# First stage of a trunk kernel: latents ahead of context, with a written order for three k tiles

## The chip, the cores and the metric

The kernel runs on one core of a Trainium2 chip. The metric is the device time of one execution in microseconds (us); the reader sees the median of three runs and one execution that the hardware profiler recorded. Engines are named as in the profile: PE is TensorE (PEld its weight loads), DVE is VectorE, ACT is ScalarE, POOL is GpSimd and SP is SyncE, which issues nearly all DMA transfers here. A "q" behind an engine's name means its sequencer.

## The reference

A trunk of two layers works on 256 latent tokens `x` and 256 context tokens `ctx`, both of width 2048. Of each layer, what matters here is its beginning:

```python
shift, scale, gate = jnp.split(silu_c @ w_mod[l] + b_mod[l], 3, axis=-1)
shift_c, scale_c, gate_c = jnp.split(silu_cc @ w_mod[l] + b_mod[l], 3, axis=-1)

h = rmsnorm(x, g_pre[l]) * (1.0 + scale[:, None]) + shift[:, None]
h_c = rmsnorm(ctx, g_pre[l]) * (1.0 + scale_c) + shift_c
proj = h @ w_in[l]
proj_c = h_c @ w_in[l]
```

Both streams are normalised over the 2048 features, scaled and shifted by a modulation computed from `silu(c)` and `silu(c_ctx)`, and projected with the same weights `w_in`. The columns of the projection feed a gated MLP (parts called au, av, ag), windowed attention (q, k, v, bg) and a Fourier branch (cx, cg); their outputs are joined and projected by `w_out`. All of it is in float32.

## The kernel before

Activations lie transposed: features on the 128 partitions, in 16 tiles of 128 features (k tiles, `KT`), and tokens along the free axis, 256 latents and then 256 context tokens (`T` = 512, `S` = 256). `yo[k]` holds x and ctx of k tile k. Each float32 product is made from three passes of a reduced type: every operand is split into a high and a low part (`hh`/`hl` for activations, `whi`/`wlo` for weights), and `mm3` multiplies high by high, high by low and low by high. ACT makes a high part, DVE the low one. `W`, the `Stream`, loads weight blocks of 128x1024 into `raw` (three buffers) and splits them into `whi` and `wlo`; `emitting(512)` does so by halves.

The first stage of layer 0 runs over the k tiles. For every k tile, the modulation's scale and shift come from 2 MB of `w_mod` (`in_wsl_dram`), read in four quarters by the generator `mod_start`: one `next` issues the loads, four multiply a quarter each on PE (`ps_mod`, L169), one transposes on DVE, the last multiplies once more (`ps_modc`, L178) and writes `gs` (scale) and `sh` (shift). Odd k tiles load into the buffers mg, mgl, hh, hl (from k tile 9 on yo in place of hh, hl), even ones into mraw, mraw, macc, vv. `make_h` then forms h on DVE (L507), its high part on ACT (L511) and its low part on DVE (L516), and PE multiplies it into av (four tiles of 128 tokens, `start_av`) and into three heads of au (`start_au`). All these sums stay in PSUM for the whole stage.

Ahead of the stage stand the statistics. SP loads all of x and ctx, ACT squares each `yo[k]` (L1238), and PE sums the squares over the partitions by products with ones (L1242), which go to four column groups of the array in turn. The sums are copied, added up (L1254), scaled on DVE, raised to -1/2 on POOL, and spread to all partitions by a broadcast product (`bcast`, `ps_rb`). Products with zeros (`warm`, L474, `ps_idle`) fill PE between these pieces; I call them fillers.

PE's order is the order in which the program is written (`manual_schedule`), and in the first stage the same holds for DVE, ACT and SP. Each queue runs in order: an instruction that waits holds up all that stand behind it on its engine. Two constants shape the steps: up to k tile `EARLY` a step computes the modulation of the next k tile, from there on that of the one after the next; in step `EARLY` itself there are two. `LOADS` and `SPLITS` say how many weight blocks are loaded and split in each step.

## Time and profile before

| what | value |
|---|---|
| median of 3 runs (lowest to highest) | 1136.24 us (1136.19 to 1136.27) |
| the profiled execution | 1136.23 us |
| its span, first to last instruction | 1134.5 us |
| PE busy in the span | 1122.2 us (99%) |
| first projection (av) of k tile 0 | at 24.57 us |
| first projection of k tile 1 | at 33.66 us |
| first stage's last au product ends, next unit starts | at 138.51 us |

A timeline row reads: start, time from the first start to the last end, engine, line, operation, output<-inputs, shape, count, and in brackets how long the engine had been idle and what released it. Matmuls are pipelined and their ends modelled, so a matmul's duration is longer than the distance to the next one; distances of starts tell PE's pace. A row of windows gives for each engine the busy time and the number of instructions.

### The profile page before, as it was taken

To read this page: it belongs to the slowest core of one execution; us is meant where nothing else is said; L and a number is where in the kernel's file an instruction comes from. 1 tells how busy PE (TensorE), PEld (TensorE's weight loads), DVE (VectorE), ACT (ScalarE), POOL (GpSimd) and SP (SyncE) were. 2 spreads that over 40 slices of the span, in tenths; PEclk is the share of its full clock that TensorE was granted. 3 is DMA by queue.
4 is the path that set the end of the run, shared out by engine and by line. 5 is a ranking of instruction groups with operands and counts; after the bars stand their busy time and mean duration, and the time that the engine had idled before them with its cause. 6 is when DMAs were issued, how large, how long until landed. Compare 5 with 4: busy or idle time off the path is not lost.

```text
span 1134.5 us, 16841 instructions
## 1 busy us (share of the span) xinstructions
PE 1122.2 (99%) x6332; PEld 932.0 (82%) x6335; DVE 879.7 (78%) x1480; ACT 514.6 (45%) x933; POOL 33.0 (3%) x39
## 2 busy tenths in 40 slices
PE   8999999999999999999999999999999999999997
PEld 3567788888898888888888888988898988888885
DVE  1545499999987887789999994397788689868884
ACT  5322422322325667632533323366555369856551
POOL 0000000000000000000000000205000000000001
PEclk9999999999999999999999999999999999999998
DMA  9999666556655343356466664269656686555872
GB/s 353 400 390 403 241 204 191 179 189 219 207 168 184 113 136 117 116 188 188 166 203 212 215 196 157 62 192 240 203 182 208 214 273 191 175 163 188 299 261 74
DMA packets 72659, 234.28 MB, mean 207 GB/s; under 512 B 8449, under 2 KB 11393, under 8 KB 72577
## 3 DMA queue, kind: packets, MB, share of 16 engines
q1 hardware_dynamic: 70272, 231.11, 61.1%
q0 software_dynamic: 2304, 2.10, 1.2%
q8 instruction: 49, 0.80, 0.3%
q14 instruction: 34, 0.27, 0.1%
HBM read 231.08 MB, written 2.10 MB: 206 GB/s over the span
## 4 chain that ended last, share of the span: by engine, by line
PE 97%; DMA 2%; DVE 0%; SPq 0%; ACT 0%; issue 0%; POOL 0%; DVEq 0%; POOLq 0%
PE ps_t L428 14%; PE ps_t L429 14%; PE ps_t L430 14%; PE ps_t L545 10%; PE ps_t L546 5%; PE ps_y L428 3%; PE ps_y L430 3%; PE ps_y L429 3%; PE ps_mod L169 2%; PE ps_av L428 2%; PE ps_cx L428 2%; PE ps_cx L430 2%; PE ps_cx L429 2%; PE ps_av L429 2%; PE ps_av L430 2%; PE ps_tp L924 2%
## 5 line engine op out<-in xcount | busy, mean ns | idle before, releaser
L403 ACT CAST whi<-raw 128x1024 fp32r<-128x1024 f32 (+1 forms) x216 | 224.0, 1041 | 328.8 <-PE ps_t L429 182.1
L408 DVE TENSOR_TENSOR wlo<-raw,whi 128x1024 fp32r<-128x1024 f32 (+1 forms) x216 | 260.4, 1210 | 62.9 <-ACT whi L403 61.5
L428 PE MATMUL ps_t<-hh,whi 128*128 128x512 f32 (+1 forms) x704 | 268.4, 381 | 0.0
L430 PE MATMUL ps_t<-hh,wlo 128*128 128x512 f32 (+1 forms) x704 | 267.8, 380 | 0.0
L429 PE MATMUL ps_t<-hl,whi 128*128 128x512 f32 (+1 forms) x704 | 267.6, 380 | 0.0
L207 DVE SCALAR_TENSOR_TENSOR macc<-mraw,cs,macc 128x512 f32<-128x512 f32 x360 | 249.1, 746 | 17.1 <-DMA mraw<-in_wmod_dram 17.1
L545 PE MATMUL ps_t<-hh,whi 128*128 128x512 f32 x448 | 163.7, 403 | 0.0
L430 PEld LDWEIGHTS ps_t<-hh,wlo 128*128 128x128 f32 x704 | 132.5, 188 | 25.2
L428 PEld LDWEIGHTS ps_t<-hh,whi 128*128 128x128 f32 x704 | 132.5, 188 | 24.7 <-issue 0.8
L429 PEld LDWEIGHTS ps_t<-hl,whi 128*128 128x128 f32 x704 | 132.5, 188 | 23.4
L546 PE MATMUL ps_t<-hh,wlo 128*128 128x256 f32 x448 | 125.7, 281 | 0.0
L545 PEld LDWEIGHTS ps_t<-hh,whi 128*128 128x128 f32 x448 | 84.3, 188 | 19.1 <-issue 0.5
L546 PEld LDWEIGHTS ps_t<-hh,wlo 128*128 128x128 f32 x448 | 84.9, 189 | 0.5 <-issue 0.5
L511 ACT ACTIVATE hh<-w2k,sh 128x256 fp32r<-128x256 f32 x48 | 21.8, 502 | 79.2 <-DVE w2k L507 79.2
L428 PE MATMUL ps_y<-whi,hh 128*128 128x512 f32 x104 | 41.3, 397 | 0.0
L430 PE MATMUL ps_y<-whi,hh 128*128 128x512 f32 x104 | 40.6, 391 | 0.0
L429 PE MATMUL ps_y<-wlo,hh 128*128 128x512 f32 x104 | 40.5, 390 | 0.0
L428 PE MATMUL ps_av<-whi,hh 128*128 128x512 f32 x96 | 39.9, 416 | 0.6 <-ACT hh L511 0.6
L428 PE MATMUL ps_cx<-whi,hh 128*128 128x512 f32 x96 | 38.7, 403 | 0.0
L429 PE MATMUL ps_av<-wlo,hh 128*128 128x512 f32 x96 | 37.9, 395 | 0.0
L429 PE MATMUL ps_cx<-wlo,hh 128*128 128x512 f32 x96 | 37.4, 389 | 0.0
L445 ACT CAST w2k<-ps_tp 128x512 fp32r<-128x512 f32 x40 | 23.4, 584 | 23.2 <-PE ps_scc L429 12.7
(398 smaller groups left out, 1858.6 us busy)
## 6 DMA issues: line engine op xcount, KB each, us to landing
raw<-in_win_dram SPq DMA_DIRECT2D x160, 512.0 KB, 4.2
mraw<-in_wmod_dram SPq DMA_DIRECT2D x128, 512.0 KB, 4.5
raw<-in_wout_dram SPq DMA_DIRECT2D x60, 512.0 KB, 4.4
mraw<-in_wsl_dram SPq DMA_DIRECT2D x16, 512.0 KB, 7.2
yo<-in_xT_dram SPq DMA_DIRECT2D x16, 256.0 KB, 5.2
macc<-in_wsl_dram SPq DMA_DIRECT2D x8, 512.0 KB, 7.8
vv<-in_wsl_dram SPq DMA_DIRECT2D x8, 512.0 KB, 7.7
mg<-in_wsl_dram SPq DMA_DIRECT2D x8, 512.0 KB, 8.0
```

The source lines that it names most:

```text
L169: PE.matmul(ps[32 * kk:32 * kk + 32, 0:n], cpad[:, kg * 4 + kk], ws[kk], start=kg == 0, stop=kg == 3, tile_position=(0, 32 * kk))
L207: V.scalar_tensor_tensor(out=acc[:, s], in0=w[:, kk % 2], scalar=c, in1=acc[:, s], op0=ALU.mult, op1=ALU.add)
L403: A.copy(ph, rc)
L408: self.last = V.tensor_tensor(out=pl, in0=rc, in1=ph.bitcast(F32), op=ALU.subtract)
L428: PE.matmul(ps, st[0], mv[0], start=start, stop=False)
L429: PE.matmul(ps, st[0], mv[1], start=False, stop=False)
L430: PE.matmul(ps, st[1], mv[0], start=False, stop=stop)
L445: A.copy(hi, src)
L511: first = A.activation(h_of(l, k, sl)[0], t[:, sl], AF.Identity, bias=sh[l][:, k, s:s + 1])
L545: PE.matmul(ps, w[0], h, start=k == 0, stop=False)
L546: PE.matmul(ps[:, 0:S], w[1], h[:, 0:S], start=False, stop=k == KT - 1)
L924: PE.transpose(tp[:, (2 * j + b) * P:(2 * j + b + 1) * P], src, ident)
```

## The change

x and ctx are loaded as separate streams, in pairs of k tiles: `yo[2i]` holds the latents of k tiles 2i and 2i+1, `yo[2i+1]` their context, and `x_of` finds them in layer 0. The latents come first, then half of the first weight block and the first modulation, then the context, then the second modulation. c is loaded by ACT's queue. The statistics are made for the latents alone; the context's squares and sums follow behind the latents' projection of k tile 0, each product with a filler ahead of it, and its statistics end behind that (`context`, called from the step of k tile 0). The first two weight blocks are loaded by halves (`loading`). The steps of k tiles 0, 1 and 2 have orders of their own. `EARLY` is 7 in place of 4, and `MIDDLE` is gone.

```diff
-    LOADS = [1, 2, 0, 2, 1, 1, 1, 1, 1, 0, 2, 0, 1, 1, 1, 0]
+    LOADS = [0, 2, 0, 2, 1, 1, 1, 1, 1, 0, 2, 0, 1, 1, 1, 0]
-    MIDDLE, EARLY = 3, 4
+    EARLY = 7
...
+    def x_of(l, k, s):
+        if l:
+            return yo[k][:, s * S:(s + 1) * S]
+        return yo[k // 2 * 2 + s][:, k % 2 * S:(k % 2 + 1) * S]
...
                 if k == 0:
-                    start_av(0, range(nt))
-                    take_in(3)
+                    start_av(0, (0, 1))
+                    state["context"](lambda: take_in(1))
+                    av.extend(mm_ps("av") for _ in range(2))
+                    au.extend(mm_ps("au") for _ in range(2))
+                    take_in(2)
+                    make_h(0, 0, rb0[:, CTX], [1])
+                    take_in(1)
                     e = W.emitting(512)
                     next(e)
+                    take_in(1)
                     next(e)
-                    take_in(2)
+                    next(state["w0"])
+                    start_av(0, (2,))
+                    mod_in(1)
+                    start_av(0, (3,))
+                    make_h(0, 1, rb0, [0, 1], state["w0"])
                     take(0, (1,))
-                    start_au(0, (0,))
-                    h_next()
-                    list(e)
-                    start_au(0, (1,))
-                    warm(au[2], 3)
+                    start_au(0, (0, 1))
+                elif k == 1:
+                    au.append(ms_ps("au"))
+                    start_av(1, (0, 1))
+                    take_in(5)
+                    avs = W.emitting(512)
+                    next(avs)
+                    start_av(1, (2,))
+                    take_in(1)
+                    start_av(1, (3,))
+                    make_h(0, 2, rb0, [0, 1], avs)
...
+        for i in range(8):
+            load_x(i, 0)
+            if i == 5:
+                DMA.dma_start(raw, const[:, 0:NFIRST])
+        DMA.dma_start(vecs, vec)
+        loads = [W.loading() for _ in range(2)]
+        next(loads[0])
+        m = mod_start(0, 1)
+        next(m)
+        for i in range(8):
+            load_x(i, 1)
+        made[1] = mod_start(1, 1)
+        next(made[1])
...
+        sq = mm_ps("rs2")
+        for i in range(8):
+            if i % 4 == 0:
+                warm(idle, 6)
+            square(sq, 0, i)()
...
+        r0 = sums_of(sq)
...
+        warm(idle, 2)
+        next(m)
+        spread(r0, 0)
+        for _ in range(2):
+            warm(idle, 3)
+            next(m)
+        warm(idle, 3)
+        next(m)
+        next(m)
+        warm(idle, 3)
+        sq = mm_ps("rs2")
+        first = square(sq, 1, 0)
+        list(m)
+        warm(idle, 4)
+        make_h(0, 0, rb0[:, LAT], [0])
...
+        def context(between):
+            first()
+            for i in range(1, 8):
+                product = square(sq, 1, i)
+                warm(idle, 1)
+                product()
+            r = sums_of(sq)
+            between()
+            spread(r, 1)
```

`square` squares one `yo` on ACT and returns the product with ones; `sums_of` copies the sums, adds them up and starts the root; `spread` broadcasts the result into one half of `rb0`.

Where the context's squares stand on ACT shows in its order. Before, all squares stand ahead of the copy of the sums, and k tile 0's h (`hh`) follows for both streams:

```order
L1238 ACTIVATE w2k_191<-yo_15_75 128x512
L1238 ACTIVATE w2k_194<-yo_16_76 128x512
L1243 CAST identr_89<-w2k_117 128x128
L1244 COPY cst_79<-w2k_117 128x34
L1246 COPY w2k_199<-ps_rs_33_123 128x512
L1261 COPY acc_241<-ps_rb_236 128x512
L403 CAST whi_264<-raw_209 128x512
L511 ACTIVATE hh_67_267<-w2k_269,sh_28_92 128x256 x2
```

After, one square of the context stands ahead of the latents' h and seven behind it, then the copy of their sums:

```order
L1301 COPY acc_149<-ps_rb_211 128x256
L1284 ACTIVATE w2k_242<-yo_2_62 128x512
L525 ACTIVATE hh_68_256<-w2k_258,sh_28_92 128x256
L1284 ACTIVATE w2k_271<-yo_4_64 128x512
L1284 ACTIVATE w2k_275<-yo_6_66 128x512
L1284 ACTIVATE w2k_279<-yo_8_68 128x512
L1284 ACTIVATE w2k_283<-yo_10_70 128x512
L1284 ACTIVATE w2k_287<-yo_12_72 128x512
L1284 ACTIVATE w2k_291<-yo_14_74 128x512
L1284 ACTIVATE w2k_295<-yo_16_76 128x512
L1291 COPY w2k_299<-ps_rs_65_241 128x512
```

What moved is the context's half of the statistics: from ahead of the first h to behind the latents' part of it.

On PE, with the sums of squares: before, a filler (join), then four products (ps_rs, from the squares w2k) to the four column groups, then fillers again, four times over.

```order
L474 MATMUL ps_idle_124<-join_95 128x512
L1242 MATMUL ps_rs_33_123<-w2k_143,ones_80 32x512
L1242 MATMUL ps_rs_33_123<-w2k_152,ones_80 32x512
L1242 MATMUL ps_rs_33_123<-w2k_155,ones_80 32x512
L1242 MATMUL ps_rs_33_123<-w2k_158,ones_80 32x512
L474 LDWEIGHTS join_95
L474 MATMUL ps_idle_124<-join_95 128x512
```

After, the latents' eight stand like that, but the context's stand on PE behind the first two av projections of k tile 0 (ps_av, from the weights whi, wlo and from hh, hl):

```order
L439 MATMUL ps_av_263<-whi_200,hl_69_257 128x512
L1286 MATMUL ps_rs_65_241<-w2k_242,ones_80 32x512
L483 LDWEIGHTS join_95
L483 MATMUL ps_idle_148<-join_95 128x512
L1286 MATMUL ps_rs_65_241<-w2k_271,ones_80 32x512
L483 LDWEIGHTS join_95
L483 MATMUL ps_idle_148<-join_95 128x512
L1286 MATMUL ps_rs_65_241<-w2k_275,ones_80 32x512
```

What moved is half of the products, from ahead of the first projection to behind its first half, and no two of that half are neighbours.

On SP, with the loads of the weight blocks (raw) and of the modulations of k tiles 2 (mraw, macc, vv) and 3 (mg, mgl and on): before,

```order
L383 DMA raw_298<-in_win_dram 128x1024
L162 DMA mraw_363<-in_wsl_dram 128x1024
L162 DMA mraw_365<-in_wsl_dram 128x1024
L162 DMA macc_367<-in_wsl_dram 128x1024
L162 DMA vv_369<-in_wsl_dram 128x1024
L383 DMA raw_371<-in_win_dram 128x1024
L383 DMA raw_373<-in_win_dram 128x1024
L162 DMA mg_445<-in_wsl_dram 128x1024
```

and after, at the same place of SP's queue, where raw_112 is the first block and raw_142 the second:

```order
L392 DMA raw_112<-in_win_dram 128x512
L162 DMA mraw_376<-in_wsl_dram 128x1024
L162 DMA mraw_378<-in_wsl_dram 128x1024
L162 DMA macc_380<-in_wsl_dram 128x1024
L162 DMA vv_382<-in_wsl_dram 128x1024
L392 DMA raw_142<-in_win_dram 128x512
L383 DMA raw_385<-in_win_dram 128x1024
L383 DMA raw_387<-in_win_dram 128x1024
L162 DMA mg_464<-in_wsl_dram 128x1024
```

What moved is the second halves of the first two blocks, to either side of the third modulation; the fourth block, raw_387, takes over the buffer of raw_112 and stands ahead of the next modulation as raw_373 did.

More of the change, by code (lines that the diff above doesn't have):

```diff
@@ L384, in load, with loading @@
             self.raws.append(r)
+        def loading(self):
+            n = len(self.raws)
+            r = sb([P, 1024], F32, "raw", NRAW)
+            self.raws.append(r)
+            for c in (slice(0, 512), slice(512, 1024)):
+                DMA.dma_start(r[:, c], self.src[n][:, c])
+                yield
         def emitting(self, cut=1024):
@@ L506, in make_h @@
             rsl = slice((s - streams[0]) * S, (s - streams[0] + 1) * S)
-            V.scalar_tensor_tensor(out=t[:, sl], in0=yo[k][:, sl], scalar=gs[l][:, k, s:s + 1],
+            V.scalar_tensor_tensor(out=t[:, sl], in0=x_of(l, k, s), scalar=gs[l][:, k, s:s + 1],
                                    in1=rb[:, rsl], op0=ALU.mult, op1=ALU.mult)
@@ L588, in layer @@
         ytmp = (lambda k: y1.get(k)) if last else ysl
-        av = [mm_ps("av") for _ in range(nt)]
-        au = [mm_ps("au") for _ in range(2)] + [ms_ps("au") for _ in range(1 - l)]
+        av = [mm_ps("av") for _ in range(2)]
+        au = [mm_ps("au") for _ in range(2 * l)]
         ws_ = {}
@@ L621, in layer @@
         if l == 0:
-            made = {}
+            mod0 = state["made"]
             def mod_in(k, n=5):
                 if k < KT:
-                    g = made.setdefault(k, mod_start(k, 1))
+                    g = mod0.setdefault(k, mod_start(k, 1))
                     for _ in range(n):
@@ L647, in layer @@
                     take(k)
-                if k <= EARLY:
+                if 0 < k <= EARLY:
                     take_in(1)
+                if k == 1:
+                    next(state["load"])
                 if k >= EARLY:
@@ L659, in layer @@
                     next(e)
-                    take_in(2)
-                    take(0, (1,))
-                    start_au(0, (0,))
-                    h_next()
-                    list(e)
-                    start_au(0, (1,))
-                    warm(au[2], 3)
-                elif k < MIDDLE:
-                    start_av(k, range(nt // 2))
-                    if k == 2:
-                        list(e)
-                    take_in(2 if k == 1 else 4)
-                    start_av(k, range(nt // 2, nt))
-                    take_in(1)
-                    if k == 1:
-                        splits()
-                        take_in(2)
-                        e = W.emitting(512)
-                        next(e)
-                        next(e)
-                    start_au(k, (0,))
-                    h_next()
-                    start_au(k, (1,))
-                    if k == 1:
-                        ahead = W.next()
-                        ws_[2] = W.next()
-                        start_au(0, (2,))
-                    start_au(k, (2,))
+                    next(state["w0"])
@@ new lines, in layer @@
+                    start_av(0, (2,))
+                    mod_in(1)
+                    start_av(0, (3,))
+                    make_h(0, 1, rb0, [0, 1], state["w0"])
+                    take(0, (1,))
+                    start_au(0, (0, 1))
[9 more added lines that the diff above has]
+                    make_h(0, 2, rb0, [0, 1], avs)
+                    aus = W.emitting(512)
+                    next(aus)
+                    next(aus)
+                    list(avs)
+                    list(e)
+                    start_au(1, (0, 1))
+                    ahead = W.next()
+                    ws_[2] = W.next()
+                    start_au(0, (2,))
+                    start_au(1, (2,))
+                elif k == 2:
+                    start_av(2, range(nt))
+                    list(aus)
+                    take_in(5)
+                    start_au(2, (0,))
+                    h_next()
+                    start_au(2, (1, 2))
@@ L1225, in trunk_kernel, with load_x @@
         first_stage.enter_context(tc.manual_schedule(engines={EN.DVE, EN.Activation, EN.SP}))
-        DMA.dma_start(ct, cT)
-        for k in range(KT):
-            DMA.dma_start(yo[k], xT[k])
+        made = state["made"] = {}
         raw = w2k([P, NFIRST])
-        DMA.dma_start(raw, const[:, 0:NFIRST])
-        DMA.dma_start(vecs, vec)
+        A.dma_start(ct, cT)
+        def load_x(i, s):
+            DMA.dma_start(yo[2 * i + s].rearrange("p (j t) -> p j t", j=2), xhalf[s, i // 2][:, i % 2 * 2:i % 2 * 2 + 2])
+        for i in range(8):
+            load_x(i, 0)
+            if i == 5:
+                DMA.dma_start(raw, const[:, 0:NFIRST])
+        DMA.dma_start(vecs, vec)
+        loads = [W.loading() for _ in range(2)]
[6 more added lines that the diff above has]
+        next(made[1])
+        next(loads[1])
+        next(loads[0])
         V.memset(wz, 0.0)
@@ L1234, in trunk_kernel, with square @@
         V.tensor_copy(cpad[:, :, 0:2], cs)
-        sq, idle = mm_ps("rs2"), mm_ps("idle")
-        for k in range(KT):
+        idle = mm_ps("idle")
+        rb0 = sb([P, T], F32, "acc")
+        def square(sq, s, i):
             q = w2k([P, T])
-            A.activation(q, yo[k], AF.Square)
-            if k % 4 == 0:
-                warm(idle, 6)
-            c = slice(32 * (k % 4), 32 * (k % 4) + 32)
-            PE.matmul(sq[c], ones[:, 0:32], q, start=k < 4, stop=k >= KT - 4, tile_position=(0, 32 * (k % 4)))
@@ L1243, in trunk_kernel @@
-        A.copy(identr, raw[:, 0:P])
-        A.copy(cst[:, 0:NFIRST - P], raw[:, P:])
-        row = w2k([P, T])
-        A.copy(row, sq)
-        m = mod_start(0, 1)
-        next(m)
-        W.load()
-        next(m)
-        warm(idle, 2)
-        ps = ms_ps("rs")
-        for j in range(4):
-            PE.matmul(ps[:, j:j + 1], row[:, j * P:(j + 1) * P], cc("sel")[:, 0:1], start=True, stop=True)
-        r0 = rstd_cols(ps[:, 0:4], 4, D)
-        next(m)
-        next(m)
-        warm(idle, 1)
@@ L1259, in trunk_kernel, with sums_of @@
-        rb = bcast(r0, 4)
-        rb0 = sb([P, T], F32, "acc")
-        A.copy(rb0, rb)
+            A.activation(q, yo[2 * i + s], AF.Square)
+            c = slice(32 * (i % 4), 32 * (i % 4) + 32)
+            return lambda: PE.matmul(sq[c], ones[:, 0:32], q, start=i < 4, stop=i >= 4,
+                                     tile_position=(0, 32 * (i % 4)))
+        def sums_of(sq):
+            row = w2k([P, T])
+            A.copy(row, sq)
+            ps = ms_ps("rs")
+            for j in range(2):
+                for i in range(2):
+                    PE.matmul(ps[:, j:j + 1], row[:, (2 * i + j) * P:(2 * i + j + 1) * P], cc("sel")[:, 0:1],
+                              start=i == 0, stop=i == 1)
+            return rstd_cols(ps[:, 0:2], 2, D)
@@ new lines, in spread @@
+        def spread(r, s):
+            rb = bcast(r, 2)
+            A.copy(rb0[:, s * S:(s + 1) * S], rb[:, 0:S])
+        sq = mm_ps("rs2")
+        for i in range(8):
+            if i % 4 == 0:
+                warm(idle, 6)
+            square(sq, 0, i)()
+            if i == 5:
+                A.copy(identr, raw[:, 0:P])
+                A.copy(cst[:, 0:NFIRST - P], raw[:, P:])
+        r0 = sums_of(sq)
+        e = W.emitting(512)
+        next(e)
+        next(e)
+        warm(idle, 2)
@@ L1264, in trunk_kernel @@
         warm(idle, 3)
+        sq = mm_ps("rs2")
+        first = square(sq, 1, 0)
         list(m)
         warm(idle, 4)
-        e = W.emitting(512)
-        next(e)
-        make_h(0, 0, rb0, [0, 1], e)
-        list(e)
+        make_h(0, 0, rb0[:, LAT], [0])
+        state["w0"] = e
+        def context(between):
[7 more added lines that the diff above has]
+            spread(r, 1)
+        state["context"] = context
+        state["load"] = loads[1]
         layer(0)
```

## The prediction

> **What bounds the kernel now.** I read the page's busy times and chain first, then the windows of the opening, then its timeline row by row, then windows cut at the steps of the first stage.

> ```profile
> span 1134.5 us, 16841 instructions
> PE 1122.2 (99%) x6332; PEld 932.0 (82%) x6335; DVE 879.7 (78%) x1480; ACT 514.6 (45%) x933; POOL 33.0 (3%) x39
> PE 97%; DMA 2%; DVE 0%; SPq 0%; ACT 0%; issue 0%; POOL 0%; DVEq 0%; POOLq 0%
> ```

> PE carries the chain from end to end. Whatever delays PE's real work in the opening delays the end by as much, since nothing later waits for anything but PE. The profiled execution took 1136.23 us, its span plus 1.73, and the median of the runs is 1136.24, so I add to that.

> ```profile
> 0.00:10.00 10.00, 7.86 (x21) 1.85 (x21) 1.13 (x6) 6.25 (x10) 0.20 (x4) 1.00 0.80 268
> 10.00:20.00 10.00, 9.75 (x71) 3.55 (x71) 0.16 (x1) 6.23 (x12) 0.81 (x1) 1.00 1.05 399
> 20.00:24.50 4.50, 3.79 (x35) 1.92 (x32) 1.85 (x7) 1.60 (x4) 0.21 (x1) 1.00 1.02 399
> 24.50:34.00 9.50, 8.51 (x62) 4.76 (x63) 4.52 (x12) 2.45 (x7) 0.00 (x0) 1.00 1.04 406
> ```

> Columns: window, PE, PEld, DVE, ACT, POOL, granted clock, DMA share, GB/s. The busy PE of the first 24.5 us is mostly fillers; the transfers run at their rate of about 400 GB/s.

> ```profile
> 1.19 8.74 SPq L1228 DMA_DIRECT2D yo<-in_xT_dram  x16
> 6.27 9.49 ACT L1238 ACTIVATE w2k<-yo 128x512 f32<-128x512 f32 x14 [0.55 <-DMA yo<-in_xT_dram]
> 16.90 0.58 ACT L1246 COPY w2k<-ps_rs 128x512 f32<-128x512 f32 x1 [0.83 <-PE ps_rs L1242]
> 18.95 0.16 DVE L456 TENSOR_SCALAR rs_a<-ps_rs 128x4 f32<-128x4 f32 x1 [15.86 <-PE ps_rs L1254]
> 19.19 1.03 POOL L459 TENSOR_TENSOR rs_b<-rs_a,mhalf 128x4 f32<-128x4 f32 x1 [18.74 <-DVE rs_a L456]
> 20.27 1.16 PE L480 MATMUL ps_rb<-identr,rs_b 128*128 128x128 f32 x8
> 21.36 0.64 PE L169 MATMUL ps_mod<-vv,kt 128*32 128x256 f32 x8
> 21.93 0.82 PE L474 MATMUL ps_idle<-join 128*128 128x512 bf16 x3
> 23.49 0.88 DVE L507 SCALAR_TENSOR_TENSOR w2k<-yo,gs,acc 128x256 f32<-128x256 f32 x2
> 24.57 0.50 PE L428 MATMUL ps_av<-whi,hh 128*128 128x512 f32 x1 [0.63 <-ACT hh L511]
> 26.46 0.40 PE L428 MATMUL ps_av<-whi,hh 128*128 128x512 f32 x1
> 27.16 0.39 PE L428 MATMUL ps_av<-whi,hh 128*128 128x512 f32 x1
> 30.05 0.62 ACT L403 CAST whi<-raw 128x512 fp32r<-128x512 f32 x1 [4.62 <-DMA raw<-in_win_dram]
> 33.66 0.50 PE L428 MATMUL ps_av<-whi,hh 128*128 128x512 f32 x1
> ```

> Sixteen squares follow the landings of x. The statistics run in series (copy, DVE, POOL, broadcast at 20.27), the last quarter of the first modulation is multiplied at 21.36, and the first projection starts at 24.57. The second k tile starts at 33.66; I call that S1. From there PE has no gap, so S1 and the length of the steps behind it decide.

> **The change, part by part.**

> *Latents first.* The squares in the 9.49 us row come 0.68 apart, so the eighth of sixteen starts at 6.27 + 5 x 0.68 = 9.7 and the last at 15.1. The latents alone are eight squares; c no longer stands first in SP's queue (1.19 becomes about 0.74), and the constants between the loads cost some 0.2: the last latent square starts near 9.4. From the last square to the broadcast it took 20.27 - 15.1 = 5.2; I take the same, 14.5. Half a broadcast is 0.6, to 15.1. Then three times three fillers (0.65 by the difference of three in the filler rows of six and of three, with 0.05 to turn) and a quarter of the modulation (0.57, from 21.36 to 21.93, so 0.6) put the last quarter at 15.1 + 3 x 0.7 + 2 x 0.6 = 18.4. From there to the first projection is 24.57 - 21.36 = 3.2: 21.6, against 24.57. It gains 3 us, not the 5 that the halved load would allow, because of the fillers. The modulation's data is no limit: the row of its last piece below lands at 20.65, and 2 MB of context (5.2 us at 400 GB/s) move behind it.

> *Context statistics on PE's path.* Before, the sum products stand four by four on PE; after, each of the context's eight stands alone, with a filler ahead of it, behind the first two projections of k tile 0 (the order's rows under the change). They moved from a time in which PE waited for loads to behind real work.

> ```profile
> 1.90 2.74 PE L474 MATMUL ps_idle<-join 128*128 128x512 bf16 x6 [1.90 <-DVE join L1232]
> 8.60 1.47 PE L474 MATMUL ps_idle<-join 128*128 128x512 bf16 x6
> 9.99 1.40 PE L1242 MATMUL ps_rs<-w2k,ones 128*32 128x512 f32 x8
> 10.35 0.14 PEld L1242 LDWEIGHTS ps_rs<-w2k,ones 128*32 128x32 f32 x2 [0.20 <-ACT w2k L1238]
> 11.32 0.98 PEld L474 LDWEIGHTS <-join 128*128 128x128 bf16 x6 [0.84 <-issue]
> ```

> Four products (two instructions each) to four column groups take 1.40 together, 0.35 each. One that comes alone, the fourth at 10.35, holds PE until the filler's load at 11.32: 0.97. Fillers are 0.217 apart ((1.47 - 0.82) / 3), the sixth starts at 8.60 + 5 x 0.217 = 9.69, and the product behind it at 9.99: 0.30. I take the lone one, since in the new order every product is alone: 8 x 0.97 + 7 x 0.30 = 9.9. The other end is 8 x 0.35 + 7 x 0.30 = 4.9. [...]

> The six projections ahead took 26.46 - 24.57 = 1.9 with both streams' low parts; with one stream some 1.5. The products run from 23.1 to 33.0. ACT is not what they wait for: the seven squares that stand behind the latents' h take at most 0.63 each, from about 21.6 to 26.

> *From the sums to S1.* The copy of the sums starts right behind the last product (16.90), the broadcast at 20.27: 3.4, of which some 0.2 was a filler; 3.2, so 36.2. Half a broadcast 0.6, its copy 0.4, then 23.49 to 24.57 again 1.1: k tile 0's context projections start at 38.3. Up to S1 PE has twelve projection matmuls (av and au of k tile 0) at 0.23, by (27.16 - 26.46) / 3, so 2.8; the modulation's second product takes 0.3, and PE waits an estimated 0.5 for DVE, which has the transpose and a weight's low half ahead of the scales. S1 is 41.9, 8.2 later than 33.66.

> *The steps.* One window per k tile of before, from the second on:

> ```profile
> 33.66:42.14 8.48, 8.48 (x65) 5.31 (x65) 5.64 (x13) 3.66 (x7) 0.00 (x0) 1.00 1.03 401
> 42.14:49.51 7.37, 7.37 (x63) 4.70 (x61) 2.70 (x9) 0.85 (x3) 0.00 (x0) 1.00 1.03 409
> 49.51:56.98 7.47, 7.47 (x62) 4.91 (x62) 5.47 (x12) 3.19 (x5) 0.00 (x0) 1.00 1.02 383
> 56.98:66.18 9.20, 9.20 (x94) 5.64 (x92) 2.88 (x9) 1.84 (x3) 0.00 (x0) 1.00 1.00 353
> 66.18:73.20 7.02, 7.02 (x65) 5.18 (x62) 4.61 (x11) 1.85 (x3) 0.00 (x0) 1.00 1.03 410
> 73.20:80.09 6.89, 6.89 (x63) 5.07 (x61) 3.69 (x10) 1.85 (x3) 0.00 (x0) 1.00 1.04 402
> 80.09:86.97 6.88, 6.88 (x62) 5.07 (x61) 3.76 (x11) 1.94 (x4) 0.00 (x0) 1.00 1.02 406
> ```

> Up to `EARLY` a step takes 7.4 (the modulation's second product stands by itself, with a turn of PE on either side), the step that holds two modulations 9.2, later ones 6.9. `EARLY` goes from 4 to 7: steps 5 and 6 become 7.45, step 7 becomes 9.2, step 4 falls to 7.45. That is 3 x 7.45 + 9.2 = 31.55 against 9.2 + 7.02 + 6.89 + 6.88 = 29.99: +1.6. Step 1 no longer splits a modulation but waits for the third au weight's split, which now stands behind tile 2's h on ACT and DVE; I estimate +0.6 for it (bounds: -0.3 with no wait, +1.0). Steps 2 and 3 stay. Sum +2.2.

> *The queue of loads.* On SP the fourth weight block (raw_387) stands ahead of the third modulation (mg_464 and on), as before; what moved is the work that frees its buffer. raw has three buffers, so raw_387 needs raw_112 free, and the second half of raw_112 is now split behind the context's h, near 42; before, its low half was done at 25.68 + 0.68.

> ```profile
> 13.66 6.99 DMA vv<-in_wsl_dram
> 25.68 0.68 DVE L408 TENSOR_TENSOR wlo<-raw,whi 128x512 fp32r<-128x512 f32 x1
> 27.41 1.06 SPq L383 DMA_DIRECT2D raw<-in_win_dram  x2
> raw<-in_win_dram SPq DMA_DIRECT2D x160, 512.0 KB, 4.2
> ```

> The issue of 27.41 slips to about 42, SP and everything behind it stand until then, and the block lands 4.2 later, at 46.3; 2 MB of modulation follow in 5.2, at 51.5. PE wants them in step 2, behind twelve matmuls: 41.9 + 9.1 + 2.8 = 53.8. So it is hidden by 2.3 us. Later the transfers need per step 2.1 MB of modulation (four times 512 KB) and about 0.44 MB of weights, 6.3 us at 400 GB/s against steps of 6.9 and more; I cost it at nothing, between 0 and +3.

> *Small things.* c moves to ACT's queue ahead of its table load; a second set of statistics adds one POOL and one DVE instruction, already in the 3.2. Sum: +8.2 + 2.2 = +10.4, so 1136.2 + 10.4 = 1146.6 us.

> **The rivals.**

> 1. The products overlap across the fillers, at 0.35: 5 us less, 1141.6. For it: four together do take 1.40. Against it: the lone 0.97.
> 2. The stalled queue reaches PE: the third modulation is late, by up to 3 us, 1149. For it: a lead of only 2.3 us. Against it: 51.5 is already a late estimate.
> 3. The clock. Six fillers took 2.74 at 1.90 and 1.47 at 8.60, so PE starts at half its pace although 1.00 is shown as granted. From 33 to 38.3 PE has only short pieces to do; if it fell back, the twelve matmuls up to S1 at 0.43 in place of 0.23 add 2.4: 1149.0. Against it: its longest idle stretch there is about 1 us. [...]
> 4. Not slower: the context's sums finish as fast as its data comes. The first modulation's last piece landed at 20.65 behind all of x; the same bytes and a quarter MB more put the context's last landing near 20.9. A square (0.63) and a lone product (0.97) later it is 22.5, and S1 is 22.5 + 8.9 = 31.4 (8.9 is 41.9 - 33.0), 2.2 earlier, which the steps' +2.2 just eat: 1136.2. It decides at a last product that ends by 22.5; the order has the first one start behind projections that I expect at 21.6, and for a gain over 0.2% it would have to end by 20.2, before the data is there.

> **How the numbers follow.** Chances: the forecast 0.62 (its own range 1144 to 1149, from the +-0.5 at each of some five joints), rival 1 0.14, rival 2 0.10, rival 3 0.06, rival 4 0.08, of which half for under 1134. A measurement of this kernel tells 0.2%, 2.3 us, from no change. The range reaches from rival 1 less 0.6 to rivals 2 and 3 plus 1: 1141 to 1150. Slower 0.92, same 0.04, faster 0.04.

> **What would show it.** First av near 21.6; the context's products 1.28 apart, the last near 33; av of the second k tile near 41.9; SP idle from about 36 to 42; steps 5 and 6 at 7.4 and step 7 at 9.2; from there to the end as before. I am wrong if the products come 0.65 apart, if PE waits for a modulation in steps 2 to 8, or if fillers run at 0.43.

## The result: slower by 1.2%, and the profile after

| what | before | after |
|---|---|---|
| median of the runs (lowest to highest) | 1136.22 us (1135.96 to 1136.27) | 1149.97 us (1148.71 to 1151.58) |
| ratio after to before, 95% interval | | 1.0122 (1.0105 to 1.0140) |
| the profiled execution | 1136.23 us | 1150.72 us |
| first projection of k tile 0 | 24.57 us | 22.14 us |
| first projection of k tile 1 (S1) | 33.66 us | 42.22 us |
| end of the first stage, first `ps_t` product | 138.51 us | 148.58 us |

The forecast was 1146.6: the side was right, the size 3.4 us short. 1149.97 lies above the forecast's own range, 1144 to 1149, and only 0.03 inside the whole one, 1141 to 1150. The executions after differ by 2.9 us among themselves, those before by 0.3.

The page of the kernel after, its span, busy times and the head of the chain of work:

```profile
span 1148.9 us, 16867 instructions
PE 1133.8 (99%) x6343; PEld 932.4 (81%) x6343; DVE 880.7 (77%) x1482; ACT 514.7 (45%) x936; POOL 34.4 (3%) x40
PE 92%; DVE 5%; DMA 2%; issue 1%; POOL 0%; ACT 0%; DVEq 0%; POOLq 0%
```

PE is as busy as before, but the chain is no longer all PE: DVE and DMA are in it with 7%. The opening, row by row from the timeline of PE, and one row of SP's queue:

```profile
22.14 0.50 PE L437 MATMUL ps_av<-whi,hh 128*128 128x512 f32 x1 [0.64 <-ACT hh L525]
23.78 1.04 PE L1286 MATMUL ps_rs<-w2k,ones 128*32 128x512 f32 x2
24.76 0.39 PE L483 MATMUL ps_idle<-join 128*128 128x512 bf16 x1
32.86 1.05 PE L1286 MATMUL ps_rs<-w2k,ones 128*32 128x512 f32 x2
36.67 0.71 PE L489 MATMUL ps_rb<-identr,rs_b 128*128 128x128 f32 x4 [0.47 <-POOL rs_b L468]
38.90 0.50 PE L437 MATMUL ps_av<-whi,hh 128*128 128x512 f32 x1
42.22 0.39 PE L437 MATMUL ps_av<-whi,hh 128*128 128x512 f32 x1
27.86 14.58 SPq L383 DMA_DIRECT2D raw<-in_win_dram  x2
```

The latents' projections start at 22.14. The context's eight sum products take from 23.78 to 33.9 (1.30 from one to the next), the broadcast stands at 36.67, the context's first projection at 38.90, and k tile 1 starts at 42.22. SP's queue stands at the fourth weight block for the 14.58 of its row, and the third modulation's loads, next in it, are issued from 42.49. The windows of the steps, one per k tile from the second on (those of steps 1, 4, 7 and 8), and at the end the stretch from k tile 9 to the end of the stage:

```profile
42.22:51.09 8.87, 8.47 (x65) 5.24 (x64) 5.42 (x14) 3.31 (x7) 0.00 (x0) 1.00 0.89 337
65.87:73.12 7.25, 7.25 (x62) 4.88 (x61) 2.57 (x9) 1.12 (x3) 0.00 (x0) 1.00 1.03 412
87.61:96.82 9.21, 9.21 (x95) 5.64 (x93) 4.11 (x10) 2.67 (x5) 0.00 (x0) 1.00 0.94 324
96.82:103.85 7.03, 7.03 (x66) 5.17 (x62) 4.67 (x12) 1.85 (x3) 0.00 (x0) 1.00 1.03 410
103.85:148.58 44.73, 44.73 (x356) 33.28 (x355) 21.62 (x55) 14.09 (x24) 0.00 (x0) 1.00 0.91 343
```

S1 is 8.56 later, and the steps behind it take 148.58 - 42.22 = 106.36 against 138.51 - 33.66 = 104.85, 1.51 more. So the stage ends 10.07 later; 10.4 was forecast. The rest of the 14.49 between the two profiled executions arises behind the stage, where the order of the instructions is the same. The timelines of PE, first product behind the stage and the sums at the boundary of the layers, before and then after; after also shows a product that waits, and two rows of DVE's timeline that lead to it:

```profile
138.51 0.39 PE L428 MATMUL ps_t<-hh,whi 128*128 128x512 f32 x1
737.56 0.50 PE L1163 MATMUL ps_rs<-cst,w2k 128*128 128x1 f32 x4
```

```profile
148.58 0.40 PE L437 MATMUL ps_t<-hh,whi 128*128 128x512 f32 x1
750.47 0.50 PE L1191 MATMUL ps_rs<-cst,w2k 128*128 128x1 f32 x4
241.86 0.39 PE L438 MATMUL ps_z<-w2k,mg 128*128 128x260 f32 x1 [0.59 <-DVE w2k L455]
240.45 0.75 DVE L207 SCALAR_TENSOR_TENSOR macc<-mraw,cs,macc 128x512 f32<-128x512 f32 x1 [1.07 <-DMA mraw<-in_wmod_dram]
241.12 0.69 DVE L455 TENSOR_TENSOR w2k<-ps_f,w2k 128x512 fp32r<-128x512 f32 x1
```

From the one to the other it took 599.05 before and 601.89 after, 2.84 more. Some 0.8 of that is the wait at 241.86 (0.59 idle, and PE's turn behind it): PE wants a low part that DVE makes at 241.12, behind a step of the next layer's modulation that waited 1.07 for its data; this is how DVE and DMA came into the chain. Before, the same low part was ready in time: the same product starts at 230.69, without a wait. The other 2.0 are in no wait: the products themselves come more slowly. From the sums at the boundary to the end of the execution it took 1136.23 - 737.56 = 398.67 before and 1150.72 - 750.47 = 400.25 after, 1.58 more, of which one instruction on POOL is 1.04 (its timeline, before and after):

```profile
738.63 0.71 POOL L459 TENSOR_TENSOR rs_b<-rs_a,mhalf 128x2 f32<-128x2 f32 x1 [3.31 <-DVE rs_a L456]
```

```profile
751.54 1.75 POOL L468 TENSOR_TENSOR rs_b<-rs_a,mhalf 128x2 f32<-128x2 f32 x1 [3.30 <-DVE rs_a L465]
```

10.07 + 2.84 + 1.58 = 14.49; of the 1.58, 0.5 is in neither POOL's instruction nor another row shown here. The experiments ask three things: are the terms of the first stage what the prediction said they are, what slows products hundreds of us behind the change, and why do the executions differ.

### The profile page after: what moved, and what is told of

It reads as the page before. It is cut to its first block, busy times and chain, and to the rows that moved or that the text cites. A ratio compares the mean times of both kernels' runs of the same rounds, so it can differ in the third digit from the quotient of the medians.

```text
span 1148.9 us, 16867 instructions
## 1 busy us (share of the span) xinstructions
PE 1133.8 (99%) x6343; PEld 932.4 (81%) x6343; DVE 880.7 (77%) x1482; ACT 514.7 (45%) x936; POOL 34.4 (3%) x40
## 4 chain that ended last, share of the span: by engine, by line
PE 92%; DVE 5%; DMA 2%; issue 1%; POOL 0%; ACT 0%; DVEq 0%; POOLq 0%
PE ps_t L437 13%; PE ps_t L439 13%; PE ps_t L438 13%; PE ps_t L559 10%; PE ps_t L560 5%; PE ps_y L437 3%; PE ps_y L439 3%; PE ps_y L438 3%; PE ps_mod L169 2%; PE ps_av L437 2%; PE ps_av L438 2%; PE ps_av L439 2%; DVE macc L207 2%; PE ps_tp L952 2%; DMA mraw<-in_wmod_dram 2%; PE ps_v L439 1%
## 5 line engine op out<-in xcount | busy, mean ns | idle before, releaser
L454 ACT CAST w2k<-ps_tp 128x512 fp32r<-128x512 f32 x40 | 23.4, 585 | 23.2 <-PE ps_scc L438 12.7
## 6 DMA issues: line engine op xcount, KB each, us to landing
raw<-in_win_dram SPq DMA_DIRECT2D x158, 512.0 KB, 4.3
mraw<-in_wmod_dram SPq DMA_DIRECT2D x128, 512.0 KB, 4.4
raw<-in_wout_dram SPq DMA_DIRECT2D x60, 512.0 KB, 4.4
mraw<-in_wsl_dram SPq DMA_DIRECT2D x16, 512.0 KB, 7.6
macc<-in_wsl_dram SPq DMA_DIRECT2D x8, 512.0 KB, 7.8
vv<-in_wsl_dram SPq DMA_DIRECT2D x8, 512.0 KB, 7.8
mg<-in_wsl_dram SPq DMA_DIRECT2D x8, 512.0 KB, 6.3
```

The costliest lines, as they stand in the source:

```text
L454: A.copy(hi, src)
```

## The experiments

Medians of the kernel before beside these runs were 1136.13 to 1136.69 us (single executions 1135.24 to 1138.61, so the 0.3 above was a quiet case). Times below are medians of the executions.

**The terms of the first stage.** Products without fillers:

```diff
                 product = square(sq, 1, i)
-                warm(idle, 1)
                 product()
```

> The changed kernel without the filler ahead of each of the context's sum products, which then stand one behind the other on PE. Theory 1 (a lone product costs 0.97 because it is alone; neighbours go to four column groups and run beside each other): eight take 2 x 1.40, held back by the last square, which ended at 25.74; the last product ends near 26.7 in place of 33.9, k tile 1 starts near 35.0 in place of 42.2, and the kernel takes 1142.8. Theory 2 (the 0.97 is the product's own cost): 8 x 0.97, only the fillers' 7 x 0.30 go, last product near 31.8, 1147.9. Theory 3 (something else would hold the start of k tile 1, the second modulation's data or a weight's split): k tile 1 starts later than 36 although the products end early.

Measured: 1142.90 us (1142.86 to 1145.41), ratio 1.0057 (1.0043 to 1.0071). The timeline of PE has all eight products in one row:

```profile
25.19 3.04 PE L1286 MATMUL ps_rs<-w2k,ones 128*32 128x512 f32 x16
```

3.04 for eight, 0.38 each, against 1.30 with the fillers between: theory 1. k tile 1 started at 37.93 in this profile and not at 35.0, because the granted clock fell to 0.50 twice, at 14.75 and at 31.82 (below); without a fall it was 34.85 (e7_sum, which has other parts undone too). So some 7 of the 8.6 us that S1 lost are the fillers that keep neighbours apart.

The length of the steps:

```diff
-    EARLY = 7
+    EARLY = 4
```

> The changed kernel with EARLY at 4 in place of 7, nothing else. Theory 1 (the longer steps cost what the windows say): steps 4 to 8 go back from 7.25, 7.25, 7.25, 9.20, 7.03 to 9.20, 7.02, 6.89, 6.89, 6.90, a gain of 1.1 us, 1148.9. Theory 2 (with the loads held up to 42 us the earlier second modulation of step 4 isn't there in time): PE waits in step 4 or 5 for its data, and the gain is lost, 1150 or more.

Measured: 1150.52 us (1148.36 to 1151.26), 1.0116 (1.0102 to 1.0129). The windows of steps 4 to 8 (the first, the last and their sum):

```profile
67.52:76.73 9.21, 9.21 (x95) 5.63 (x93) 2.86 (x9) 1.85 (x3) 0.00 (x0) 1.00 0.99 372
97.52:104.42 6.90, 6.90 (x62) 5.06 (x61) 3.61 (x10) 1.85 (x3) 0.00 (x0) 1.00 1.04 400
sum 36.90, PE 36.90 PEld 25.99 DVE 18.54 ACT 9.35 POOL 0.00; mean PE 7.38 PEld 5.20 DVE 3.71 ACT 1.87 POOL 0.00
```

36.90 against 37.98 after the change, 1.08 less as theory 1 says, and PE has no gap in them. The time does not show it: 1.1 us is less than the executions differ, and in the profiled execution a fall of the clock between 36.76 and 40.17 cost 1.3. That execution also spent 3.06 us outside its span, where the other three spent 1.72 to 1.81.

SP's wait for a weight buffer, a first try:

```diff
-    LOADS = [0, 2, 0, 2, 1, 1, 1, 1, 1, 0, 2, 0, 1, 1, 1, 0]
+    LOADS = [0, 1, 1, 2, 1, 1, 1, 1, 1, 0, 2, 0, 1, 1, 1, 0]
```

> The changed kernel with the load of the fourth weight block moved from step 1 to step 2, behind the loads of the third modulation (LOADS 0, 1, 1, 2 in place of 0, 2, 0, 2): SP no longer waits until 42 with the modulation behind it. Theory 1 (the stall is hidden, as predicted: the data landed at 52.2 and was used at 53.9): the third modulation lands near 44, steps 2 to 8 stay as they are, and the time stays at 1149 to 1150. Theory 2 (the stall's delay is paid later, through loads that run just ahead of PE from 98 to 106 and at 241): the late waits go and 0.5 to 1 us is gained.

Measured: 1151.25 us, 1.0135 (1.0121 to 1.0149). It tells nothing on the stall: SP's queue still stood from 28.27 to 44.9, since a split further down in step 1 issues that load itself when it finds it missing. Its ratio does not differ from that of the changed kernel beyond the intervals. In its profile the clock fell at 14.84 and at 38.73. The second try put the modulation's loads ahead of the weight block, on top of the kernel e12_two (below):

```diff
-                if 0 < k <= EARLY:
+                if 0 < k <= EARLY and k != 2:
                     take_in(1)
...
-    LOADS = [0, 2, 0, 2, 1, 1, 1, 1, 1, 0, 2, 0, 1, 1, 1, 0]
+    LOADS = [0, 1, 0, 2, 1, 1, 1, 1, 1, 0, 2, 0, 1, 1, 1, 0]
...
+                    mod_in(3, 1)
                     aus = W.emitting(512)
```

> As e12_two (old places, fillers in the chains), with the loads of the third modulation put ahead of the fourth weight block on SP, so that they no longer stand behind its wait for a buffer: they can start once PE has multiplied the second modulation, near 38.5. Theory 1 (the wait costs nothing, as the prediction had it): the third modulation lands near 44 in place of 52.2, steps 2 to 8 keep their lengths, and the time is that of e14. Theory 2 (it is paid later): 0.5 to 1.5 us less than e14, and no wait near 241 in the profile.

> e12_two once more, for the comparison with e13_two_ns on the same chip: 1146.2 to 1148.7 as before.

Measured: e13 1147.34 us (1146.37 to 1149.20), e14 1146.88 us (1146.23 to 1149.73). The third modulation's loads in SP's queue, e13:

```profile
35.98 0.33 SPq L162 DMA_DIRECT2D mg<-in_wsl_dram  x1
39.58 0.38 SPq L162 DMA_DIRECT2D hl<-in_wsl_dram  x1
```

In e14 the same loads were issued from 42.37 to 44.81, behind a wait of 14.45. Five to six us earlier moved nothing: the stage ended at 148.24 and 148.37, the times differ by less than the executions do, and e13 has a wait of 0.5 at the place of the 241.86 row, e14 none. The stall is hidden, and that wait comes without it too.

**Where the tiles stand.** Behind the stage the instructions and their order are the same; what the change leaves different for a product 500 us later is where its operands stand. The pool gives a tile's name its address when the name is first used, and the change uses raw, mg, hh14 and others in another order. The first byte in a partition, as the programs place them:

```
                 before, e1, e12     after, e2           e9                  e10
whi and wlo      104480 to 137248    120864 to 153632    112672 to 145440    124960 to 157728
hh0, hl0         137248              153632              145440              118688
hh14 to hl15     149536              110496              149536              110496
hh1, hl1         157728              157728              157728              157728
hh3 to hl11      174112 to 210976    the same            the same            the same
```

In the kernel after, the activations of k tiles 14 and 15 stand below the weights' parts, those of the other fourteen above. In a unit of 48 products (16 k tiles, three products each) the nine of k tiles 14, 15 and 0 come 0.229 to 0.238 apart, but for one at 0.224, and all others 0.226 or 0.227; before, all 48 come 0.226 to 0.228 apart (means over four units). Four experiments move places alone, with tiles that are made ahead of their use, in an order of their own (e1's edit, with lines left out):

```diff
         raw = w2k([P, NFIRST])
+        for tag, dt, n, bufs in ([("mraw", F32, 1024, 2), ("macc", F32, 1024, 1), ("vv", F32, 1024, 1),
...
+                                 + [(f"{h}{k}", F32R, T, 1) for k in (14, 15, 1, 12, 13, 2) for h in ("hh", "hl")]):
+            for _ in range(bufs):
+                sb([P, n], dt, tag, bufs)
```

> The changed kernel with one thing undone: its tiles stand in SBUF where they stood before the change. The change makes the first tile of each name in another order, so raw, mraw, mg, whi, wlo, acc, hh0 to hh2 and hh12 to hh15 got other addresses; here they are made ahead in the old order. The instructions are the same. Theory 1 (the slower pace from 150 to 700 us comes from where the tiles stand, since only products that read hh14, hl14, hh15, hl15, hh0, hl0 are slower, 0.229 to 0.238 apart against 0.227): all products of that stretch are 0.227 apart again, the gain is about 2 us, 1148. Theory 2 (the pace is a matter of the execution, transfers or the chip): the same products stay slow and the time stays at 1150.

> The kernel before with one thing of the change alone: its tiles stand in SBUF where the change puts them. The instructions and their order are those of before. Theory 1 (place): products that read hh14, hh15 and hh0 are slower, 0.229 to 0.238 apart, some 45 ns for each sixteen k tiles, and the time is 1136.2 + 2 = 1138.2. Theory 2: nothing moves, 1136.2.

> The changed kernel with hh14, hl14, hh15 and hl15 behind hh0 and hl0 in SBUF, so that the activations of all sixteen k tiles stand side by side (from 145440 bytes on), as in the kernel before; the weights' parts whi and wlo stand 8 KB lower than the change put them. Looked at for the distance of products from 150 to 750 us. Theory 1 (products are slower where PE goes to k tiles that stand apart from the others, below the weights, and back): all are 0.227 apart. Theory 2 (it is the weights' place that counts): k tiles 14, 15 and 0 stay at 0.229 to 0.238, or others are slower.

> The changed kernel with hh0 and hl0 beside hh14 to hl15 at the low place (110496 to 122784), below the weights. Theory 1 (the products of k tiles that stand apart are slower, and of the one behind them): k tiles 14, 15 and 0 are slower, and k tile 1, the first at the high place, too, which is at 0.227 to 0.228 in the changed kernel. Theory 2 (hh0 is slow by its own place beside wlo): k tile 0 is back at 0.227.

The same product, the first of k tile 14, four units of 48 products apart, in the timelines of PE of the kernel before, of e2, of e9 and of e10:

```profile
505.73 0.39 PE L428 MATMUL ps_t<-hh,whi 128*128 128x512 f32 x1
549.25 0.39 PE L428 MATMUL ps_t<-hh,whi 128*128 128x512 f32 x1
```

```profile
506.31 0.40 PE L428 MATMUL ps_t<-hh,whi 128*128 128x512 f32 x1
550.01 0.40 PE L428 MATMUL ps_t<-hh,whi 128*128 128x512 f32 x1
```

```profile
517.38 0.39 PE L437 MATMUL ps_t<-hh,whi 128*128 128x512 f32 x1
560.89 0.39 PE L437 MATMUL ps_t<-hh,whi 128*128 128x512 f32 x1
```

```profile
518.45 0.40 PE L437 MATMUL ps_t<-hh,whi 128*128 128x512 f32 x1
562.29 0.40 PE L437 MATMUL ps_t<-hh,whi 128*128 128x512 f32 x1
```

A unit takes 43.52 / 4 = 10.88 before, 10.925 in e2, which is the program before with the new places and nothing else, 10.88 in e9 and 10.96 in e10. In e2 from the stage's end to the boundary of the layers it took 738.97 - 138.16 = 600.81 against 599.05: 1.76 us by place alone. The profiles without the wait for DVE in that stretch agree: it takes 600.80 to 600.90 with the places of the change (e2, e3, e5, e6) and 598.94 to 599.18 with the old ones or with all k tiles on one side (before, e9, e12, e14). By time e2 is 1137.87 us, 1.0011 (1.0003 to 1.0020), 0.3 to 2.3 us slower than before. In e9, with all k tiles above the weights again, no product is slow (one execution, 1148.26). In e10 (one execution, 1151.71) k tiles 14, 15 and 0 stand apart, and those of k tile 1 and the first of k tile 2 are slower too, at 0.229 to 0.236: the slowness goes on for one or two k tiles past the return. Theory 1 holds in all four profiles. e1 removed the slow pace as well (0.226 or 0.227 everywhere), but its time, 1149.61 us (1147.00 to 1150.74), 1.0105 (1.0089 to 1.0121), does not show the gain that was expected. In its profile the latents' first projection is 0.7 later than after the change, waits for DVE near 241 add up to 1.2 us, and POOL's instruction takes 1.72.

**Why the executions differ.** e3, e4 and e6 showed PE at about half its pace for a stretch (three fillers took 1.49 in e3 at 15.90, and 0.82 at 18.28), and a granted clock of 0.50 with it. Two fillers at two places of each chain of sums are to prevent that:

```diff
             A.copy(row, sq)
+            warm(idle, 2)
             ps = ms_ps("rs")
...
         def spread(r, s):
+            warm(idle, 2)
             rb = bcast(r, 2)
```

> The changed kernel with two fillers more at two places in each chain of sums, latents' and context's: ahead of the products that add up the rows, and ahead of the broadcast, where PE waits 0.4 to 0.7 us anyway. Nothing else. Theory 1 (the spread of 3 us between executions of the changed kernel is PE's clock, which falls to half for 3.41 us behind these chains in some executions, as it did at 14.75 and 31.82 in the kernel without fillers and at 36.76 in the one with EARLY 4): the clock stays at 1 between 8 us and the end in the profile, every execution shows a mean clock of 0.997 or more, and the median is about that of the undisturbed executions of the changed kernel, 1148.7 to 1149.2, plus up to 0.3 for the fillers. Theory 2 (the spread is later waits for data): executions above 1150 remain.

> The changed kernel itself, once more, for how its executions differ. If the parts found so far explain it: an execution that the clock's fall hits (a mean clock of 0.996 or less) takes 1150.5 or more, one without it 1148.5 to 1149.5, up to 1150.7 where GpSimd's power at the layer boundary takes 1.75 in place of 0.71 and the wait at 241 is there. If something else sets the spread, time and clock don't go together.

Measured: e5 1149.30 us (1148.68 to 1150.63), 1.0121 (1.0106 to 1.0137); e11, the changed kernel once more, 1150.81 us (1149.85 to 1151.45), 1.0124 (1.0107 to 1.0141). The windows of e11 around the fall in its profile, and of e12 at the same place with the fillers in:

```profile
29.87:33.28 3.41, 3.41 (x9) 0.60 (x8) 0.00 (x0) 0.00 (x0) 0.00 (x0) 1.00 1.03 406
33.28:36.69 3.41, 2.27 (x20) 1.54 (x20) 0.16 (x1) 0.59 (x1) 0.71 (x1) 1.00 0.20 78
36.69:40.10 3.41, 3.41 (x28) 1.46 (x27) 1.12 (x3) 1.91 (x4) 0.00 (x0) 0.50 0.00 0
```

```profile
34.09:37.51 3.42, 3.28 (x32) 1.97 (x34) 0.16 (x1) 0.53 (x2) 0.71 (x1) 1.00 0.05 20
```

The granted clock is 0.50 for 3.41 us, behind 3.41 us in which PE was busy for 2.27. The changes of the clock in one profile stand whole multiples of 3.41 us apart: the two falls of e3 17.07 (five), those of e6 23.89 (seven), and in the kernel after the record of the full clock goes from 7.87 to 1144.51, 333 times 3.4133. Windows are the stretches of that length counted from such a change. Cut otherwise they tell less: in e11 PE was busy for 2.32 of the 3.41 us from 11.34, which lie across two windows (2.73 and 3.00), and the clock held. In the kernel after's own profile the windows of the chain fell otherwise over the work, were busy for 2.74 and 2.94, and the clock held:

```profile
31.77:35.18 3.41, 2.74 (x11) 0.83 (x9) 0.00 (x0) 0.59 (x1) 0.00 (x0) 1.00 0.68 264
35.18:38.59 3.41, 2.94 (x41) 1.73 (x40) 0.64 (x2) 0.62 (x2) 0.70 (x1) 1.00 0.01 4
```

A fall costs 1.3 to 1.4 us: from the first projection to S1 it takes 20.05 to 20.10 without one and 21.38 to 21.47 with one (e4, e6, e9, e11). Of eight profiled kernels with the change's chains and no added fillers, five had a fall, at the latents' chain (e3, e6) or the context's (e3, e4, e6, e9, e11); of the six with the fillers none. The rest of e11's theory does not hold: an execution with a mean clock of 0.998 takes 1151.04, above the 1150.7 allowed, and e5 still spreads over 2 us. So the clock is one part of the spread. Two more things differ between the profiles: POOL's power at the boundary of the layers (0.71 in six, 1.56 to 1.78 in ten, among them e2, the program before with other places) and the wait for DVE at the place of the 241.86 row (0.3 to 1.2 us in eight of the sixteen). POOL's counts in the time: from the sums at the boundary to the end of the span it takes 396.9 to 397.5 in the six, 398.1 to 398.4 in the ten. That they also differ between executions of one program is not shown: the two programs that were profiled twice (after and e11, e12 and e14) have the long power both times, and the wait both times or not at all. What decides the two is open.

**The parts together.** First with four parts undone (e7), then with the context's products moved as well (e8, whose further edit is shown in part):

```diff
         spread(r0, 0)
+        sq = mm_ps("rs2")
+        products = [square(sq, 1, i) for i in range(5)]
         for _ in range(2):
...
-        warm(idle, 4)
+        for product in products[:4]:
+            product()
         make_h(0, 0, rb0[:, LAT], [0])
+        products += [square(sq, 1, i) for i in range(5, 8)]
...
```

> The changed kernel with four parts undone together: old places of the tiles, EARLY 4, no filler between the context's products, fillers in the chains. If the parts add up: k tile 1 starts at 42.2 - 7.1 + 0.2 = 35.3, the steps behind it take 104.85 as before plus 0.4 in step 1, so the stage ends 2.0 later than before's 138.51, the pace and the clock are those of before, and the time is 1136.4 + 2.0 = 1138.4. If the parts hide one another or the loads hold the earlier start (the third weight block landed at 36.2): 1140 or more.

> As e7_sum, and the context's squares of k tiles pairs 0 to 4 stand ahead of the latents' h on ACT, the sum products of pairs 0 to 3 stand together in place of the four fillers ahead of the first projection, and those of 4 to 7 together behind the first two projections. Theory 1: the last product ends near 25.1 in place of 33.9, k tile 1 starts near 33.4, the stage ends within 0.5 of before's 138.5, 1136.5 and no faster, since what the latents gain (2.4 at the first projection) the context's chain of 8.3 us behind its last product takes back. Theory 2: the loads (2 MB of modulation and a weight block that land up to 36.2) hold step 0 or 1, 1138 or more.

Measured: e7 1139.51 us (1138.12 to 1140.93), 1.0031 (1.0019 to 1.0043), S1 at 34.85, the stage's end at 140.10, 1.6 behind before's; 1.1 over its forecast; its profiled execution, 1140.93, has POOL at 1.73 and a wait of 0.8 for DVE at the place of the 241.86 row. e8 1136.95 us (1136.17 to 1138.73), 1.0009 (1.0000 to 1.0018), S1 at 33.46 and the stage's end at 138.69: the parts add up, and the best version of this order that was tried is no faster than the kernel before. What is left with these parts undone is the trade that the change makes: first projections 2.2 earlier, the context's chain behind them.

Last, the changed kernel with the two things undone that the prediction had no term for, old places (as e1) and fillers in the chains (as e5):

> The changed kernel with the two things undone that the prediction had no term for: tiles at their old places, and fillers in the two chains so that the clock doesn't fall. Everything that the prediction spoke of stays. If its terms were right and these two made the rest: 1136.4 + 10.1 to 10.4 = 1146.5 to 1146.8, mean clocks of 0.997 and more. If not: 1148 or more.

Measured: 1147.41 us (1146.21 to 1148.65), 1.0097 (1.0082 to 1.0112), mean clocks 0.998; again in e14, 1146.88 us, 1.0099 (1.0082 to 1.0116). By the ratios that is 11.0 and 11.2 over before, against 10.4 forecast; e12's profile ends the stage at 148.43, 9.92 later than before's, takes 747.40 - 148.43 = 598.97 to the boundary, as before, and has POOL at 1.63 there, 0.92 more than before's. The expected 1146.5 to 1146.8 is missed by less than the executions differ.

## Why the prediction was right and where it was wrong

- **Latents first**, 21.6 forecast: 22.14. The broadcast, put at 14.5 (9.4 + 5.2 is 14.6), stood at 15.03, and the half us stayed. The last latent square started at 10.1 and not at 9.4: in ACT's timeline two copies of constants (9.00 to 9.40) stand among the squares.
- **Context statistics on PE's path**, eight products at 0.97 with seven fillers at 0.30, 9.9 us: 23.78 to 33.9 by the rows above, 10.1. The choice of the lone product's price over the overlapping one was the choice that decided the size, and e3 shows the other price, 0.38, when neighbours stand together. After the change a product took 1.30 with its filler; what makes it dear there no row shows.
- **From the sums to S1**, broadcast 36.2, context at 38.3, S1 41.9: 36.67, 38.90 and 42.22. S1 moved by 8.56 where 8.2 was forecast.
- **The steps**, +2.2: +1.51. Step 1 became 0.4 longer and not 0.6, and steps 4 to 6 took 7.25 and not 7.45. `EARLY`'s own price is 1.08 (e4), 1.6 was forecast.
- **The queue of loads**, nothing: confirmed. The third modulation landed 1.7 before its use, and taking the stall away changes nothing (e13 against e14). Rival 2 is out.
- **Sum for the stage**: +10.4 forecast, +10.07 measured. It is closer than its parts, which is luck in part: S1 cost 0.36 more than forecast and the steps 0.69 less. Rival 1 and rival 4 are out by the same rows.
- **The step that failed** is the one that closed the sum: "from there to the end as before". S1 and the steps were taken to decide alone, since "nothing later waits for anything but PE", and everything behind the stage was put at nothing. In the profiled execution it was 4.42 of the 14.49. The operands of the products behind the stage aren't at the same place, and place alone makes 1.76 us (e2) in that stretch. On top come 0.8 for the wait for DVE near 241 and 1.04 on POOL, which with place and the stage make up 13.7 of the 14.5; the other 0.8 is not assigned. That the change itself brings the wait and POOL's longer time is not shown. With the old places and the chains' clock held, the same change costs 11.0 (e12; 9.3 to 12.7 by its interval), and the forecast's 10.4 lies in that interval.
- **Rival 3, the clock**, was put aside because the longest idle stretch is about 1 us. It happens nevertheless, at the place named, in some executions, and costs 1.3 to 1.4 us and not 2.4; the profiled execution of the changed kernel had none, so it is no part of the 14.49. It is cheaper than forecast because the fall lasts 3.41 us, and for much of that time PE has only short pieces to do. The argument from the longest gap was the error: the windows ahead of these falls had PE busy for 2.27 to 2.47 of 3.41 us, and no wait over 0.7.

## What to carry to other kernels

A change at the front of a program can move the addresses of everything that is first used behind it; compare the places of the operands, not only the order of the instructions, before writing "the rest as before". Small products for the array's column groups were cheap side by side here (0.38 each) and dear one by one with a filler between (1.30). And where a chain of small steps leaves PE half idle, ask how busy it is over any few us (here at most 2.47 of 3.41 ahead of a fall), and not only how long its longest gap is.
